# Output products of a hybrid decoder step: from marks along the recurrence to groups of three, ordered both ways by columns

## The chip, the core and the metric

One core of a Trainium2 chip runs one program. The metric is the device time of one execution in microseconds (us). Its engines are named as in the profile: PE (TensorE, with PEld for its weight loads), DVE (VectorE), ACT (ScalarE), POOL (GpSimd) and SP (SyncE, whose queue issues most DMAs here). Each engine takes its instructions in the order in which they stand in the program.

## The reference

One layer of a decoder. The input is normalised and projected, and the columns of the projection go to four groups of heads and a gate. Only the third group (RWKV-7) and the end matter here:

```
def step(S, inp):
    r_t, w_t, k_t, v_t, kk_t, a_t = inp
    sa = jnp.einsum('bhij,bhj->bhi', S, -kk_t)
    S = (S * w_t[:, :, None, :] + sa[..., None] * (kk_t * a_t)[:, :, None, :]
         + v_t[..., None] * k_t[:, :, None, :])
    return S, jnp.einsum('bhij,bhj->bhi', S, r_t)
...
o = jnp.concatenate([oa, ob, oc, od], axis=-1) * jax.nn.silu(gate)
y = x + rms_norm(jnp.einsum('bte,ed->btd', o, w_out), norm_post)
```

The prompt has 2048 tokens; a sample group of 8 sequences of 8 tokens goes through the same weights. The width is 1024, of which the recurrence has 256 (4 heads of 64).

## The kernel before, in words

The first two thirds of the program (input projection, attention, the other head groups) are not touched; the instructions of every engine stand there in the same order before and after. The last part, from about 1250 us of the trace on, is the one that counts: the recurrence and the output projection.

**The recurrence** runs over 16 blocks of 128 tokens, each as two chunks of 64. The generator `rw_prompt` (L1446) gives its steps out one by one. For block i they are: `rw_chain(i)` (L1312), the products that carry the state from chunk to chunk; `rw_tri(i+1)` (L1273), the rest of the triangular inverse of the next block; `rw_norm(i)` (L1397), the group norm of block i, which ends in `out_prep` (L1532), the scaling of token tile i into two f16 halves `o_h`; and `front(i+2)`, which is `rw_prep` (L1105), `rw_mats` (L1182) and `rw_base` (L1252) of the block after the next.

**The round trip to DRAM.** `rw_mats` ends with a small table of diagonal blocks, `r_de` (L1214, DVE). SP writes it to a DRAM tile `zd` (L1217) and reads it back spread over the partitions into `r_zr` (L1221). `rw_base` inverts the 16x16 blocks with it: 15 pairs of small DVE instructions, `r_x16w` (L1262) and `r_x` (L1263), each pair on the result of the one ahead.

**The chain.** For each chunk PE makes `rc` from state `r_Z` and `r_W` (8 products), ACT copies `r_gs`, PE multiplies by `r_TT` (4), ACT scales the result back into `r_Z`, PE multiplies by `r_BK` (4), DVE adds the decayed state (L1372, the new `r_Z`), and PE makes the output with `r_ET` (4), which ACT copies to `r_y`.

**The output** (`out_tile`, L1568) of a tile of 128 tokens is 48 products `acc<-wo,o_h` (L1584) of 512 columns: two halves of 512 output columns, each 8 steps k of three f16 products. ACT scales and squares each half (`o_y`, `o_j`), DVE makes the norm (`o_ss`, `oq`, `o_y`), POOL adds the input (`o_x`, L1599), SP stores.

**What sets the order.** The framework places each engine's instructions by a model of time of its own, which orders whatever the program leaves free. The program adds edges with `issue_after`: the instructions in the block come behind a given one on the same engine. `rw_chain` appends the last product of each of its steps to a list, `spine` (`mark`, L1321), and the three products of a step k of an output tile come behind an entry of that list:

```
ins = spine[(KT * g + k) * len(spine) // (2 * KT)] if spine else None
```

The edge goes one way: nothing holds a product of the recurrence behind an output product. In the loop (L1864) tile i-2 goes out in iteration i, from the second iteration on, after the step of `rw_chain`; one step of the sample's recurrence (`rw_sample`, L1439) follows each of the first five steps of the prompt's. Tiles 14, 16 (the sample's 64 tokens) and 15 are left for the end, in this order.

Of the kernel before, what the change touches and what calls it, by code (L numbers as in the profile page):

```python
# [23 lines left out]
P = 128  # L24
# [12 lines left out]
class Marked:  # L37


    def __init__(self, eng):  # L40
        self.eng, self.done = eng, []

    def matmul(self, *a, **k):
        r = self.eng.matmul(*a, **k)
        self.done.append(r.ins)
        return r

    def transpose(self, *a, **k):
        r = self.eng.transpose(*a, **k)
        self.done.append(r.ins)  # L50
        return r


class Part:


    def __init__(self, ctx, tc, ins, outs):
# [3 lines left out]
        self.PE = Marked(nc.tensor)  # L61
# [1250 lines left out]
    def rw_chain(self, b, S=None):  # L1312
# [8 lines left out]
        mark = lambda ins: smp or self.spine.append(ins.ins)  # L1321
# [13 lines left out]
        for q in range(b.ch):  # L1335
# [3 lines left out]
            for k in range(2):  # L1339
# [7 lines left out]
                mark(ins)  # L1347
# [7 lines left out]
            mark(ins)  # L1355
# [5 lines left out]
            if not smp:  # L1361
# [7 lines left out]
                mark(ins)  # L1369
# [6 lines left out]
            mark(ins)  # L1376
# [69 lines left out]
    def rw_prompt(self, pool):  # L1446

        bs = {}
        self.spine = []
# [118 lines left out]
    def out_tile(self, i, h, sc, pool, psum, spine=()):  # L1568
# [7 lines left out]
        for g in range(2):  # L1576
            sl = slice(512 * g, 512 * g + 512)
            a = psum.tile([P, 512], F32, name="acc", bufs=ACB)
            c = 0
            for k in range(KT):  # L1580
                ins = spine[(KT * g + k) * len(spine) // (2 * KT)] if spine else None
                for e, f in ((0, 0), (0, 1), (1, 0)):
                    with self.tc.issue_after(ins) if ins and e == f else ExitStack():
                        nc.tensor.matmul(a[:n].rearrange("p (c n) -> p c n", c=4), h[:, k, e], self.wo[:, 4 * g:4 * g + 4, k, f, :],  # L1584
                                         start=c == 0, stop=c == 3 * KT - 1)
                    c += 1
            y = pool.tile([P, 512], F32, name="o_y", bufs=OB[3])
# [4 lines left out]
        nc.vector.tensor_tensor(ss[:n, 2:3], ss[:n, 0:1], ss[:n, 1:2], op=ALU.add)  # L1592
        nc.vector.tensor_scalar(ss[:n, 2:3], ss[:n, 2:3], 1.0 / D, 1e-6, op0=ALU.mult, op1=ALU.add)
        self.rsqrt(pool, ss[:n, 3:4], ss[:n, 2:3], n, 1, "oq")
        for g, y in enumerate(ys):
            sl = slice(512 * g, 512 * g + 512)
            nc.vector.scalar_tensor_tensor(y[:n], y[:n], ss[:n, 3:4], self.npo[:n, sl], op0=ALU.mult, op1=ALU.mult)  # L1597
# [173 lines left out]
def program(tc, ins, outs):  # L1771
    with ExitStack() as ctx:
# [68 lines left out]
        with ph2:  # L1841
# [22 lines left out]
            for i in range(RB, 16):  # L1864
                mark = len(p.spine)
                n = min(-((t - 14) // (16 - i)), i - LAG - t)
                for k in range(4):
                    next(seq, 0)
                    if k in SK:
                        next(smp, 0)  # L1870
# [110 lines left out]
```

## Time and profile before

| what | value |
|---|---|
| median of 3 runs | 1844.46 us (1842.14 to 1845.57) |
| the profiled execution, its own time | 1846.33 us |
| span of its trace | 1844.5 us |
| busy over the span | PE 1497.3 us (81%), DVE 1448.1 (79%), ACT 902.1 (49%), POOL 811.6 (44%) |
| granted clock of TensorE, mean | 0.881 of 2.4 GHz |

The shares are means over stages with different limits. What a change in the last stage is worth has to be read from the waits of that stage.

### The profile page before, as it was taken

What the parts mean: (1) busy time and instruction counts of PE and PEld (TensorE: products, weight loads), DVE (VectorE), ACT (ScalarE), POOL (GpSimd) and SP (SyncE); (2) the same over time, 40 slices, a digit from 0 to 9 for tenths busy, and PEclk for the clock granted to TensorE, in tenths of its full rate; (3) what the DMA queues carried; (4) which work ended last, traced back from release to release, by engine and by line L of the source; (5) the groups of instructions that cost most, each with busy time, mean ns of one, the idle gap of its engine ahead of it and who ended that gap; (6) DMA issues with size and microseconds to landing.
All of it is one profiled execution on the core that took longest, in us unless ns stands there. A gap on an engine that the chain in (4) does not pass through costs nothing.

```text
span 1844.5 us, 33323 instructions
## 1 busy us (share of the span) xinstructions
PE 1497.3 (81%) x10956; PEld 844.9 (46%) x10956; DVE 1448.1 (79%) x4619; ACT 902.1 (49%) x2211; POOL 811.6 (44%) x887
## 2 busy tenths in 40 slices
PE   4889888987789788878894899657688887887887
PEld 2445644444344344434442456446455454554443
DVE  7797639988899899889896754376878887888865
ACT  3455746655556566657772222243344454444333
POOL 3441326736668877443344454261324333333312
PEclk9999998999899899989996999875777887887889
DMA  4422144575445655464447877635223233333221
GB/s 147 128 91 93 28 116 117 125 149 117 111 111 139 152 141 146 106 145 115 86 104 199 274 250 238 205 96 163 73 66 100 81 105 93 92 86 102 66 72 58
DMA packets 300898, 225.33 MB, mean 122 GB/s; under 512 B 192531, under 2 KB 248565, under 8 KB 300213
## 3 DMA queue, kind: packets, MB, share of 16 engines
q1 hardware_dynamic: 288388, 184.85, 37.4%
q10 hardware_dynamic: 8496, 24.76, 4.7%
q0 software_dynamic: 3840, 13.61, 2.6%
q8 instruction: 86, 1.41, 0.3%
q14 instruction: 88, 0.71, 0.1%
HBM read 130.04 MB, written 53.24 MB: 99 GB/s over the span
## 4 chain that ended last, share of the span: by engine, by line
DVE 34%; PE 21%; DMA 15%; issue 8%; POOL 4%; ACT 3%; SPq 1%; ACTq 0%; POOLq 0%; DVEq 0%
PE acc L206 7%; DMA r_zr<-zd 5%; DVE a_mx L365 4%; PE acc L1584 4%; DVE a_e L389 4%; DMA a_wt<-a_w 3%; DVE r_x L1263 2%; DVE r_x16w L1262 2%; DVE a_w L395 2%; DMA zd<-r_de 2%; PE ss L511 2%; DVE r_W L1177 1%; PE pf L530 1%; POOL a_e L388 1%; POOL a_w L395 1%
## 5 line engine op out<-in xcount | busy, mean ns | idle before, releaser
L206 PE MATMUL acc<-hT,w 128*128 128x512 f16 (+1 forms) x3120 | 633.6, 353 | 24.7 <-ACT pst L640 4.3
L206 PEld LDWEIGHTS <-w 128*128 128x128 f16 x3120 | 269.7, 101 | 322.3 <-issue 66.8
L368 ACT ACTIVATE a_e<-s,a_mx,sig 128x512 f32<-128x512 f32 (+3 forms) x320 | 226.9, 715 | 122.6 <-DVE a_mx L366 106.4
L1584 PE MATMUL acc<-wo,o_h 128*128 128x512 f16 (+1 forms) x816 | 225.1, 422 | 1.2 <-ACT o_y L1588 0.6
L365 DVE TENSOR_REDUCE a_mx<-s 128x1 f32<-128x512 f32 (+3 forms) x320 | 186.3, 599 | 23.4 <-PE s L361 18.7
L388 POOL TENSOR_SCALAR a_e<-a_e,a_al 128x512 f32<-128x512 f32 (+3 forms) x160 | 114.6, 731 | 148.6 <-DVE a_al L384 119.4
L389 DVE SCALAR_TENSOR_TENSOR a_e<-a_e,a_al 128x512 f32<-128x512 f32 (+3 forms) x160 | 149.3, 948 | 9.2 <-POOL a_e L388 9.0
L361 PE MATMUL s<-kh,qh 128*128 128x512 f16 (+3 forms) x320 | 105.7, 359 | 38.2 <-ACT a_e L368 35.0
L402 PE MATMUL pv<-vtok,a_wt 128*128 128x128 f16 x544 | 70.0, 230 | 64.6 <-DMA a_wt<-a_w 57.9
L392 ACT CAST a_w<-a_e 128x512 f16<-128x512 f32 (+3 forms) x160 | 86.3, 557 | 69.9 <-DVE a_e L389 63.5
L1584 PEld LDWEIGHTS <-o_h 128*128 128x128 f16 (+1 forms) x816 | 76.6, 105 | 95.1 <-issue 26.3
L395 POOL TENSOR_TENSOR a_w<-a_e,a_w 128x512 f16<-128x512 f32 (+3 forms) x80 | 90.0, 1128 | 64.4 <-ACT a_w L392 62.4
L1262 DVE TENSOR_TENSOR r_x16w<-r_zr,r_x 128x60 f32<-128x60 f32 (+18 forms) x255 | 58.8, 231 | 67.0 <-DMA r_zr<-zd 63.8
L1599 POOL TENSOR_TENSOR o_x<-o_y,o_x 128x512 f32<-128x512 f32 (+1 forms) x33 | 48.4, 1487 | 121.4 <-DVE o_y L1597 84.7
L402 PEld LDWEIGHTS <-a_wt 128*128 128x128 f16 x544 | 52.2, 104 | 91.4 <-DMA a_wt<-a_w 76.1
L395 DVE TENSOR_TENSOR a_w<-a_e,a_w 128x512 f16<-128x512 f32 (+2 forms) x80 | 76.9, 964 | 2.7 <-ACT a_w L392 2.7
L170 POOL TENSOR_TENSOR hT<-hf,hT 128x512 f16<-128x512 f32 (+1 forms) x36 | 36.5, 1022 | 88.3 <-ACT hT L168 88.2
L403 PE MATMUL pv<-vtok,a_wt 128*128 128x64 f16 x544 | 66.1, 202 | 0.0
L1263 DVE TENSOR_TENSOR r_x<-r_x,r_x16w 128x60 f32<-128x60 f32 (+18 forms) x255 | 62.4, 245 | 3.4
L368 ACT ACTIVATION_READ_ACCUMULATOR a_e<-s,a_mx,sig 128x1 f32 x320 | 64.0, 200 | 0.0
L366 DVE TENSOR_SCALAR a_mx<-a_mx,sig 128x1 f32<-128x1 f32 x320 | 59.8, 201 | 0.4
L511 PE MATMUL ss<-kv,qbd 128*32 128x256 f32 x256 | 52.5, 415 | 6.7 <-DMA kv<-in_ckv 6.5
(552 smaller groups left out, 3378.0 us busy)
## 6 DMA issues: line engine op xcount, KB each, us to landing
kv<-in_ckv SPq DMA_DIRECT2D x128, 256.0 KB
w<-in_w_in ACTq DMA_DIRECT2D x20, 512.0 KB
pc<-pst SPq DMA_DIRECT2D x40, 256.0 KB
xw<-in_xT SPq DMA_DIRECT2D x16, 512.0 KB
w<-in_w_out ACTq DMA_DIRECT2D x16, 512.0 KB
sg<-pst SPq DMA_DIRECT2D x32, 256.0 KB
r_X<-pc SPq DMA_DIRECT2D x16, 512.0 KB
r_zr<-zd SPq DMA_DIRECT2D x16, 512.0 KB
```

The lines of the kernel that those rows point to most:

```text
L206: self.nc.tensor.matmul(acc[:, :n], w16[:, k, a, :], h[:, k, e, :], start=(c == 0), stop=(c == 3 * KT - 1))
L361: ins = nc.tensor.matmul(s[:, :kn], q[:, c], kh[:, c, k0:k0 + kn], start=True, stop=True)
L365: nc.vector.tensor_reduce(mx[:, p, c:c + 1], s[:, :kn], axis=AX.X, op=ALU.max, negate=True)
L368: nc.scalar.activation(e[:, :kn], s[:, :kn], AF.Exp, scale=sig, bias=mx[:, p, c:c + 1], accum_out=l[:, p, c:c + 1])
L388: nc.gpsimd.tensor_scalar(e1[:, :kn], e1[:, :kn], al[:, p, 1:2], 0.0, op0=ALU.mult, op1=ALU.add)
L389: nc.vector.scalar_tensor_tensor(e0[:, :kn], e0[:, :kn], al[:, p, 0:1], e1[:, :kn], op0=ALU.mult, op1=ALU.add)
L395: eng.tensor_tensor(w[:, kn:], e0[:, :kn], w[:, :kn], op=ALU.subtract)
L402: ins = nc.tensor.matmul(pv[:, :P], wt[:, j], v, start=kt == 0, stop=kt == qb, skip_group_check=True)
L511: ins = nc.tensor.matmul(sp[g:g + 32, 256 * j:min(256 * j + 256, n)], self.qbd[:, m, s].rearrange("p a q -> p (a q)"), rhs, start=True, st ...
L1262: XV.tensor_tensor(w[:, :, :m], zr[:, k, :, k + 1:], x[:, :, k:k + 1].to_broadcast([P, nu, m]), op=ALU.mult)
L1263: XV.tensor_tensor(x[:, :, k + 1:], x[:, :, k + 1:], w[:, :, :m], op=ALU.add)
L1584: nc.tensor.matmul(a[:n].rearrange("p (c n) -> p c n", c=4), h[:, k, e], self.wo[:, 4 * g:4 * g + 4, k, f, :], start=c == 0, stop=c == 3 * ...
```

## The change

- `Marked`, the wrapper of PE that the recurrence's products go through, counts the columns of the products that it issues. With a generator `fill` of output products set by `begin`, it draws one group from it for every `step` columns. A group comes behind the product issued last (`self.PE.last`), and the next product of the recurrence comes behind the group (`gate`). `flush` draws what is left.
- `out_tile` no longer issues anything: it gives two generators, one for each half of the tile, which yield after each group of three products, and a function `rest` with the norm and the store. The two halves have a PSUM buffer each (before: two buffers of one name).
- The loop sends out tile i-1 (before: i-2) in iteration i: the first half between the products of `rw_chain` (a group per 300 columns), the second between those of `rw_tri`, `rw_norm` and `front` (a group per 590 columns; 220 in iteration 14, 30 in iteration 15). Tiles 16 and 15 are left for the end.
- The sample's recurrence is issued whole at the end of iteration 0.

```diff
 class Marked:
+    def begin(self, fill, step):
+        self.fill, self.cols, self.step, self.gate = fill, 0, step, fill and self.last
+
+    def issue(self, op, out, a, k):
+        with self.tc.issue_after(self.gate) if self.gate else ExitStack():
+            r = op(out, *a, **k)
+        self.gate = None
+        self.cols += math.prod(out.shape[1:])
+        self.last = r.ins
+        while self.fill and self.cols >= self.step:
+            self.cols -= self.step
+            self.gate = next(self.fill, None)
+            if self.gate is None:
+                self.fill = None
         return r
...
-    def out_tile(self, i, h, sc, pool, psum, spine=()):
+    def out_tile(self, i, h, sc, pool, psum):
...
-        for g in range(2):
-            sl = slice(512 * g, 512 * g + 512)
-            a = psum.tile([P, 512], F32, name="acc", bufs=ACB)
+        def half(g):
+            a = psum.tile([P, 512], F32, name=f"acc{g}", bufs=1)
             c = 0
             for k in range(KT):
-                ins = spine[(KT * g + k) * len(spine) // (2 * KT)] if spine else None
                 for e, f in ((0, 0), (0, 1), (1, 0)):
-                    with self.tc.issue_after(ins) if ins and e == f else ExitStack():
+                    with self.tc.issue_after(self.PE.last) if e == f else ExitStack():
...
+                if k < KT - 1:
+                    yield ins.ins
...
             for i in range(RB, 16):
-                mark = len(p.spine)
-                n = min(-((t - 14) // (16 - i)), i - LAG - t)
-                for k in range(4):
+                halves = out(i - 1) if i else (None, None, lambda: None)
+                p.PE.begin(halves[0], PACE[0])
+                next(seq, 0)
+                p.PE.flush()
+                p.PE.begin(halves[1], PACE[1 + max(i - 13, 0)])
+                for k in range(3):
+                    if i == 15 and k == 0:
+                        p.out_prep(16)
                     next(seq, 0)
...
+                p.PE.flush()
+                halves[2]()
+                drain(smp)
...
+PACE = (300, 590, 220, 30)
```

The edges move instructions on all engines. Two places on PE and one on DVE follow.

PE, a block in the middle of the prompt before, from the end of the front (`r_prk`, `r_xv`, then `rw`, `hsel` of the block after it) to the transposes of the norm (`r_yc`) and the chain's second step (`r_gs,r_TT`):

```order
L44 MATMUL ra<-r_prk,selh 64x128 x4
L49 MATMUL ra<-ident,r_xv 128x128 x2
L44 MATMUL ra<-r_X,rw_15071 32x128 x4
L44 MATMUL rl<-r_X_17157,r_NA 32x32 x8
L44 MATMUL ra<-r_L,rw_15073 128x128 x2
L44 MATMUL ra<-hsel,r_sq 128x2 x2
L44 MATMUL rl<-r_TT,r_H_17179 32x32 x8
L44 MATMUL ra<-r_L,rw_15073 128x128 x2
L49 MATMUL rl<-ident,r_yc 128x128 x2
L44 MATMUL rc<-r_gs,r_TT 64x64 x4
```

The same products of a middle block in the change, after the last products of `rw_tri`:

```order
L48 MATMUL rl<-r_X_19254,r_NA 32x32 x3
L48 MATMUL rl<-ident,r_yc 128x128 x2
L1594 LDWEIGHTS o_h
L1594 MATMUL acc_19267<-wo,o_h 128x512
...
L48 MATMUL ra<-r_X,rw_15071 32x128 x4
L48 MATMUL rl<-r_TT,r_H_19280 32x32 x8
L1561 MATMUL rl<-o_mx,onec 128x1
L48 MATMUL ra<-r_L,rw_15073 128x128
```

Before, the front's first products (`ra<-r_X,rw`, `r_L`, `hsel`) stand ahead of the norm's transposes `r_yc`; in the change they stand behind them, with a group of three in between, and the tile's `o_mx` stands ahead of `r_L`. This repeats in every block from the second to the fourteenth.

PE, the chain's steps in the change (before, the 4 products of a step stand together, and output products only between steps):

```order
L48 MATMUL rc<-r_gs,r_TT 64x64 x2
L48 MATMUL rc<-r_Z,r_BK 64x64 x3
L1594 LDWEIGHTS o_h
L1594 MATMUL acc_17099<-wo,o_h 128x512
...
L48 MATMUL rc<-r_Z,r_BK 64x64
L48 MATMUL rc<-r_Z,r_W 64x64
L48 MATMUL rc<-r_Z,r_ET 64x64 x3
```

The groups now stand inside the steps: three products before, and one behind, in the step with `r_BK`.

DVE, from `r_de` on, a middle block before:

```order
L1214 TENSOR_REDUCE r_de<-r_dg 128x64
L1409 TENSOR_REDUCE r_nm<-r_y 128x4
L1413 SCALAR_TENSOR_TENSOR r_yc<-r_nm,r_y 128x256
L1243 TENSOR_TENSOR r_sv<-r_xv,ra 128x256
L1592 TENSOR_TENSOR o_ss<-o_ss 128x1
L1593 TENSOR_SCALAR o_ss<-o_ss 128x1
L1294 TENSOR_TENSOR r_TT<-r_XY,rl 128x256
L99 TENSOR_SCALAR o_ss<-o_ss 128x1
L1420 TENSOR_REDUCE r_nss<-r_nsq 128x4
L1281 STREAM_TRANSPOSE r_X_18809<-r_TT 128x256
L100 TENSOR_SCALAR o_ss<-o_ss 128x1
L1421 TENSOR_SCALAR r_nss<-r_nss 128x4
```

And a middle block in the change:

```order
L1231 TENSOR_REDUCE r_de<-r_dg 128x64
L1260 TENSOR_TENSOR r_sv<-r_xv,ra 128x256
L1607 TENSOR_TENSOR o_ss<-o_ss 128x1
L1279 TENSOR_TENSOR r_x16w<-r_zr,r_x_19926 128x60
L1608 TENSOR_SCALAR o_ss<-o_ss 128x1
L1280 TENSOR_TENSOR r_x_19926<-r_x_19926,r_x16w 128x4x15
L116 TENSOR_SCALAR o_ss<-o_ss 128x1
L1279 TENSOR_TENSOR r_x16w<-r_zr,r_x_19926 128x4x14
```

Before, the norm of one block, the end of `rw_tri` and the norm of an output tile stand between `r_de` and the first instruction that reads `r_zr`, which is the 29th behind `r_de` in the block shown. In the change it is the third, in this block and in nearly all others.

## Rows read from the trace of the kernel before

**Rows 1.** The page's chain that ended last, whole span: shares by engine.
```profile
DVE 34%; PE 21%; DMA 15%; issue 8%; POOL 4%; ACT 3%; SPq 1%; ACTq 0%; POOLq 0%; DVEq 0%
```
**Rows 2.** Busy time by stage (us, with instructions), then granted clock, DMA share, GB/s.
```profile
core 0: us, PE busy (x) PEld busy (x) DVE busy (x) ACT busy (x) POOL busy (x), PEclk, DMA share, GB/s
1258.00:1311.00 53.00, 36.56 (x374) 30.22 (x375) 41.25 (x169) 17.12 (x53) 12.12 (x21) 0.53 0.52 156
1311.00:1753.00 442.00, 364.55 (x3210) 214.45 (x3211) 366.42 (x1431) 186.05 (x522) 154.67 (x217) 0.81 0.31 87
1753.00:1799.00 46.00, 38.97 (x355) 19.70 (x354) 28.10 (x128) 18.91 (x53) 8.83 (x11) 0.89 0.23 73
1799.00:1844.50 45.50, 33.01 (x151) 14.95 (x150) 25.60 (x98) 15.63 (x36) 10.41 (x7) 0.92 0.17 58
```
**Rows 3.** Waits of DVE from 1311 to 1753 us: us, times, longest.
```profile
DVE r_x16w L1262 <- DMA r_zr<-zd: 53.4, 13, 6.6
DVE o_o L1526 <- DMA o_o<-od: 2.3, 3, 1.0
```
**Rows 4.** SP's queue, timeline: start, us, the writes of r_de (five of 17).
```profile
1249.47 0.33 SPq L1217 DMA_DIRECT2D zd<-r_de  x1
1276.84 0.33 SPq L1217 DMA_DIRECT2D zd<-r_de  x1
1310.77 0.34 SPq L1217 DMA_DIRECT2D zd<-r_de  x1
1344.23 0.33 SPq L1217 DMA_DIRECT2D zd<-r_de  x1
1752.61 0.33 SPq L1217 DMA_DIRECT2D zd<-r_de  x1
```
**Rows 5.** The chain that ended last, one round trip: start, us, what.
```profile
1514.36 0.58 DVE r_de L1214
1514.96 2.22 DMA zd<-r_de
1517.25 6.73 DMA r_zr<-zd
1524.00 0.22 DVE r_x16w L1262
```
**Rows 6.** DVE, timeline: instructions that waited, with idle time and its releaser.
```profile
1271.67 0.45 DVE L1281 STREAM_TRANSPOSE r_XY<-r_XY 128x256 f32<-128x256 f32 x1 [0.79 <-POOL r_XY L1270]
1285.29 0.42 DVE L1420 TENSOR_REDUCE r_nss<-r_nsq 128x4 f32<-128x256 f32 x1 [0.48 <-ACT r_nsq L1419]
1787.96 0.63 DVE L1423 TENSOR_TENSOR r_yc<-r_yc,r_nrs 128x256 f32<-128x256 f32 x1
1791.60 0.43 DVE L1431 TENSOR_TENSOR r_yo<-r_yo,r_sv 128x256 f32<-128x256 f32 x1 [2.68 <-ACT r_yo L1429]
1813.60 0.16 DVE L1548 TENSOR_TENSOR o_mx<-o_mx 128x1 f32<-128x1 f32 x1 [0.64 <-ACT o_j L1547]
```
**Rows 7.** PE, timeline: products that DVE waits for, and two groups of three.
```profile
1790.28 0.44 PE L49 MATMUL rl<-ident,r_yc 128*128 128x128 f32 x2
1517.80 0.61 PE L44 MATMUL ra<-hsel,r_sq 128*128 128x2 f32 x4
1536.63 1.71 PE L44 MATMUL ra<-r_W,r_F 64*128 64x128 f32 x16
1535.88 0.82 PE L1584 MATMUL acc<-wo,o_h 128*128 128x512 f16 x3
1521.91 1.46 PE L1584 MATMUL acc<-wo,o_h 128*128 128x512 f16 x3
```
**Rows 8.** ACT, groups from 1300 us on: busy us, mean ns of one, idle before.
```profile
L1561 ACT ACTIVATE o_h<-o_o,o_sc 128x1024 f16<-128x1024 f32 (+1 forms) x17 | 19.1, 1123 | 36.1 <-DVE o_sc L1559 33.4 <-DVE r_Dp L1132 2.7
L1148 ACT ACTIVATE r_sq<-r_X,vec 128x128 f32<-128x128 f32 x24 | 8.3, 398 | 1.2 <-PE ra L44 1.2
L1529 ACT ACTIVATE o_j<-o_o 128x768 bf16<-128x768 f32 (+1 forms) x16 | 13.1, 820 | 0.3
L1206 ACT COPY r_NA<-ra 64x256 f32<-64x256 f32 x28 | 10.2, 364 | 10.7 <-PE ra L44 10.4
```
**Rows 9.** The page's DMA issues: KB each.
```profile
r_zr<-zd SPq DMA_DIRECT2D x16, 512.0 KB
```
**Rows 10.** PE, timeline: the last products, tiles 16 and 15.
```profile
1822.73 10.09 PE L1584 MATMUL acc<-wo,o_h 128*128 128x512 f16 x46 [0.29 <-ACT o_y L1588]
```

More of the change, by code (lines that the diff above doesn't have):

```diff
@@ L37, with __init__, matmul, transpose @@
 class Marked:
[L40 to L45, printed above, removed]
-        return r
[L48 to L51, printed above, removed]
+    def __init__(self, eng, tc):
+        self.eng, self.tc, self.fill, self.cols, self.step, self.last, self.gate = eng, tc, None, 0, 1, None, None
+    def begin(self, fill, step):
[11 more added lines that the diff above has]
+                self.fill = None
+        return r
+    def matmul(self, out, *a, **k):
+        return self.issue(self.eng.matmul, out, a, k)
+    def transpose(self, out, *a, **k):
+        return self.issue(self.eng.transpose, out, a, k)
+    def flush(self):
+        for _ in self.fill or ():
+            pass
+        self.fill = self.gate = None
 class Part:
@@ L1591, in out_tile, with rest @@
             ys.append(y)
[L1592 to L1597, printed above, removed]
-            eng = nc.vector if i == 15 and g else nc.gpsimd
-            eng.tensor_tensor(x[:n, sl], y[:n], x[:n, sl], op=ALU.add)
-        nc.sync.dma_start(self.o["y"][t0:t0 + n], x[:n])
+            yield ins.ins
+        def rest():
+            nc.vector.tensor_tensor(ss[:n, 2:3], ss[:n, 0:1], ss[:n, 1:2], op=ALU.add)
+            nc.vector.tensor_scalar(ss[:n, 2:3], ss[:n, 2:3], 1.0 / D, 1e-6, op0=ALU.mult, op1=ALU.add)
+            self.rsqrt(pool, ss[:n, 3:4], ss[:n, 2:3], n, 1, "oq")
+            for g, y in enumerate(ys):
+                sl = slice(512 * g, 512 * g + 512)
+                nc.vector.scalar_tensor_tensor(y[:n], y[:n], ss[:n, 3:4], self.npo[:n, sl], op0=ALU.mult, op1=ALU.mult)
+                eng = nc.vector if i == 15 and g else nc.gpsimd
+                eng.tensor_tensor(x[:n, sl], y[:n], x[:n, sl], op=ALU.add)
+            nc.sync.dma_start(self.o["y"][t0:t0 + n], x[:n])
+        return half(0), half(1), rest
     def rwkv_sample_consts(self, pool):
@@ L1854, in program, with out @@
             smp = p.rw_sample(rw, sm)
[L1856 removed]
+            def out(t):
                 if t not in p.prep:
                     p.out_prep(t)
[L1859 to L1863 removed]
+                return p.out_tile(t, *p.prep.pop(t), p.opool, ops)
             for i in range(RB, 16):
[L1865 to L1883 removed]
+                halves = out(i - 1) if i else (None, None, lambda: None)
[6 more added lines that the diff above has]
+                        p.out_prep(16)
+                    next(seq, 0)
+                p.PE.flush()
+                halves[2]()
+                drain(smp)
+            for t in (16, 15):
+                halves = out(t)
+                drain(halves[0])
+                drain(halves[1])
+                halves[2]()
 LEAD = 1500
@@ L1921 @@
 SSB = 3
-LAG = 1
 ES = 999
```

34 lines of the change are left out of this document (3 added, 31 removed).

## The prediction

> **What bounds the kernel now.** I read the page's chain of waits first, since it says which engine ended the program [rows 1]: DVE has the largest share, 34%, then PE 21% and DMA 15%. It covers the whole span, so the next view is the busy time by stage [rows 2]. From 1311 to 1753 us, 13 of the 16 blocks, PE works 364.55 and DVE 366.42 of 442 us: neither is full, and PE works at a granted clock of 0.81. What fills the rest on DVE is in the view of its waits for that stretch [rows 3]: 53.4 us, 13 times, always the first instruction that reads `r_zr`, for the DMA that brings it. SP's timeline gives the pace: the write of `r_de` to `zd` comes at 1344.23 for block 3 and at 1752.61 for block 15 [rows 4], 12 intervals in 408.4 us, 34.03 us each. Per block DVE works 366.42/13 = 28.2 us and waits 53.4/13 = 4.1 us for `r_zr`; 1.7 us are small waits. So the stage goes by the order of DVE's instructions: it is busy or waits for the round trip.
>
> The chain that ended last shows one round trip [rows 5]: `r_de` is done at 1514.94, the write lands 2.2 us later, the read takes 6.73, and the first `r_x16w` runs at 1524.00. That is 9.06 us, of which DVE waits 4.1 on average, since it makes the norm, the end of `rw_tri` and the output's norm in the other 5. These are the 28 rows that stand between `r_de` and `r_x16w` in the order before.
>
> **The change part by part.**
>
> *The round trip's cover.* The change removes and adds no arithmetic: DVE keeps its 28.2 us per block. But two-way edges put PE into the program's order. The front's first product `ra<-r_X,rw` now stands behind the norm's transposes `r_yc`, so DVE has to make `r_yc` of block i before anything of the front of i+2. The norm can then no longer stand behind that front's `r_de`. In the new order `r_de` is followed by `r_sv` and one `o_ss`, and then by `r_x16w`, which needs the transfer issued just before. Instructions of these sizes took 0.43 and 0.16 us [rows 6], so 9.06 - 0.6 = 8.5 us per block lie open. I take 8.5; PE's and ACT's work under it does not help, since the decayed state `r_Z` stands behind this wait on DVE too, and with it the rest of the chain and its groups. The transfer itself could change with what shares the queues: it is 512 KB [rows 9], and no other size of it is in the trace, so I leave it.
>
> On the size of the wait a rule can be set against rows 5. The Trainium skill ("DMA: Bandwidth & Descriptors", "Anatomy of one DMA — SWDGE (gpsimd) path") fits a transfer, on the path of POOL's software queue, by about 2.0 us and its bytes at 436 GB/s; as an estimate this gives some 2.1 us for `zd`, 3.2 us for `r_zr`, 5.3 us in all instead of 9.06, and a forecast about 45 us lower. The trace has the very transfer and disagrees for the read (6.73 us), and the sum goes by the trace.
>
> *What the norm and the front now wait for.* Before, DVE had an instruction of another step for nearly every gap. Now the steps of DVE stand one behind the other, base (i+2), norm (i), `out_prep`, front (i+3), and each answer of PE, ACT or POOL is waited for. Per block, by the nearest rows:
> - `r_XY` for POOL: 0.79 us [rows 6], on a block that had little else to do.
> - `r_nss` for ACT: 0.48 us was the wait there [rows 6]. ACT's queue now has `o_j` (0.82 us) [rows 8] of the same tile ahead of `r_nsq`; between 0.5 and 1.6, I take 1.0.
> - `r_yc` to `r_yo`: the transposes and ACT's copy left DVE idle for 2.68 us in the last block, where nothing else was to do [rows 6]; from the transposes' start at 1790.28 [rows 7] to `r_yo` at 1791.60 it is 1.3. I take 1.3, as some of the output's norm stands in between.
> - `o_mx` for `o_j`: 0.64 us [rows 6].
> - `o_sc` to `r_ss`: `o_h` (1.12 us) now stands ahead of two `r_sq` (0.40 each) on ACT [rows 8], and PE's `hsel` follows (0.61 us) [rows 7]: 2.5 us.
> - The products `ra<-r_W,r_F` (1.71 us) with a group of three ahead (0.82 us, 1.46 in the slow case) [rows 7] and ACT's copy (0.36 us) [rows 8]: 2.9 us.
> - `r_TT`, `oq` and `r_Dp`, for which no row shows a wait of this kind: nothing at best, the 0.5 us of `r_nss` each as the nearest; 1.5 us.
>
> The sum is 8.5 + 0.8 + 1.0 + 1.3 + 0.6 + 2.5 + 2.9 + 1.5 = 19.1 us, and with DVE's 28.2 the interval is 47.3 us. With only the first lower bounds (8.5, 0.8, 0.5, 0, 0.6, 1.1 for `o_h` alone, 1.7, 0) it is 41.4.
>
> *PE's clock.* PE's 364.55/13 = 28.0 us per block would fill 59% of 47 us, and 82% before. In the stretch where the trace has PE at 69%, 1258 to 1311 us, the granted clock was 0.53, half speed for most of it [rows 2]. I expect part of the stage at half speed. The parts that DVE waits for and that are PE's (some 5.5 us of the 19.1) grow by up to 0.81/0.53, which is 2.9 us; I take **50 us** per block. Half speed throughout, with groups of 1.46 us and more in front of each awaited product, bounds it at 56.
>
> *Twelve blocks*: 12 x (50 - 34.03) = **+192 us**.
>
> *The first blocks and the sample.* From the write of block 1 (1249.47) to that of block 3 (1344.23) [rows 4] it was 94.8 us, with the sample's `zd` in between. Less two intervals of 34.03 the sample cost 26.7. Before it was woven into five steps of the prompt's; now it is issued whole behind iteration 0, with its own round trip. I put it at the same 26.7, and at up to 9 more if its round trip lies open. The first of the two blocks has no output tile: 45 us, the other 50. Together 122: **+27 us**.
>
> *The tail.* From the write of block 15 to the end it was 91.9 us. Tile 14 no longer goes out last: 46 products took 10.09 us [rows 10], 0.22 each, so 48 are 10.5 us. They now stand inside the last chain, whose products wait behind them; there PE has 45.5 - 33.0 = 12.5 idle us at most [rows 2]. The gain is between 0 and 10.5; I take **-5 us**.
>
> *Queues.* Nothing is added to SP's or POOL's. On SP the store of a tile, which waits for POOL's `o_x`, stands behind the transfers `r_zr` and `r_xv` of the front, so it doesn't hold them. PSUM gives each half one buffer: a half's first group waits for ACT's reads of the half one tile ago, a whole interval earlier. Both cost nothing while a block takes more than PE's 28 us.
>
> **The sum.** 192 + 27 - 5 = 214 us on the profiled execution's 1846.33 us: 2060. The median shown is 1.9 us below that execution, so I forecast **2058 us**.
>
> **Rivals.**
>
> *Only the transfer shows.* If the waits on ACT and PE stay short, an interval is 28.2 + 8.5 + 1.7 = 38.4 us: 12 x 4.4 = 53 us, some 9 for the first two blocks, nothing for the tail, so 1907. For it: POOL and ACT have much room. Against it: DVE's next instruction now mostly stands on the answer of the one ahead.
>
> *It ends faster.* The groups inside the steps are there to fill PE's short gaps. If they set the pace, the awaited products find PE warm, the clock goes from 0.81 to near 1, and DVE's 28.2 us plus 0.8 for small waits is the interval: 13 x (34.0 - 29.0) = 65 us less, and with -10 at the tail 1770 us. It decides from the point where at least 9 us of DVE's work stand between `r_de` and `r_x16w`; the new order shows 0.6, and 5 didn't suffice before. The Trainium skill speaks for this side ("TensorE: Matmul & The Clock Gate", "HAM oscillation — how this bites in real kernels"): a loop that leaves PE idle for a wait in each round starts each round cold. By that rule the wait of 8.5 us would as well cool PE anew in every block, the opposite, and the 0.53 of rows 2 leans that way.
>
> *No change.* The engines' work is the same, and if the open waits only take the place of DVE's old ones, 4.1 + 1.7 us, the time stays at 1844. It needs gaps that the rows of the order contradict.
>
> *Half speed throughout.* An interval of 56 gives 12 x 22 = 264 us and 35 at the beginning: about 2140.
>
> **How the numbers follow.** Serial steps at 42 to 54 us have 0.80, half speed throughout 0.06, only the transfer 0.06, no change 0.03, faster 0.05. The lower end of the range is the lower bound of the interval: 12 x (42 - 34.03) = 96, +15 and -7 for the ends, 1950. The upper is the half speed case with a little more, 2150. The likeliest case lies inside, with part of the fourth; what is out is the transfer alone, no change and faster. About 0.2% is what a measurement of this kernel can tell from no change: faster 0.05, within 0.03, slower 0.92.
>
> **What would show it.** Right: the writes of `r_de` stand 45 to 54 us apart; DVE waits for `r_zr` 13 times or more, some 8 us each, 110 us in the stage where it was 53; `r_ss`, `r_yo` and `o_mx` appear among DVE's waits, for PE and ACT; DVE's own busy time per block stays near 28 us; PE's granted clock in the stage falls below 0.81. Wrong: intervals below 40 us with `r_zr` as DVE's only large wait (the transfer alone); a PE over 90% busy at a clock near 1 (the faster case); a wait of PE for the PSUM halves, or of the front for a store on SP, which I put at nothing; a first part much over 122 us, if the sample's round trip isn't covered by anything.

## The result and the profile after

The changed kernel takes **2233.78 us** (median of 4 runs, 2229.41 to 2234.28), the kernel before 1845.01: a ratio of 1.2097 with a 95% interval from 1.2064 to 1.213. The direction was right. The size was not: 2058 us was forecast, and the time lies above the range's upper end of 2150. The profiled execution took 2229.41 us with a span of 2227.6.

The page's chain of the changed kernel, shares by engine, where DVE led in [rows 1]:

```profile
PE 35%; DVE 24%; DMA 11%; issue 8%; ACT 6%; POOL 5%; SPq 1%; ACTq 0%; DVEq 0%; POOLq 0%
```

PE has changed places with DVE. The changed kernel's SP timeline shows where the time lies:

```profile
1246.16 0.34 SPq L1234 DMA_DIRECT2D zd<-r_de  x1
1382.66 0.34 SPq L1234 DMA_DIRECT2D zd<-r_de  x1
2109.59 0.33 SPq L1234 DMA_DIRECT2D zd<-r_de  x1
```

These are the writes of blocks 1, 3 and 15, to be read against [rows 4]. From block 1 to 3 it is 136.5 us (before 94.8), from block 3 to 15 726.9 us or 12 intervals of 60.58 (before 34.03), and to the end of the span 118.1 (before 91.9). The three add 41.7 + 318.5 + 26.1 = 386.3 us; the first write came 3.3 us earlier, which makes up the 383.1 us between the two profiled executions.

Busy time by stage, columns as in [rows 2], the same three stretches:

```profile
1246.16:1382.66 136.50, 86.20 (x678) 55.60 (x677) 77.84 (x300) 35.23 (x105) 23.63 (x41) 0.61 0.30 89
1382.66:2109.59 726.93, 502.92 (x3056) 260.46 (x3053) 386.87 (x1355) 178.01 (x503) 147.43 (x204) 0.63 0.18 51
2109.59:2227.65 118.06, 79.75 (x432) 36.12 (x430) 44.26 (x181) 27.96 (x71) 16.39 (x16) 0.72 0.11 37
```

Per interval DVE is busy 386.87/12 = 32.2 us and PE 41.9, at a granted clock of 0.63. DVE's waits from 1382.66 to 2109.59 us (us, times, longest) answer to [rows 3]:

```profile
DVE r_W L1224 <- ACT r_NA L1223: 61.9, 24, 3.8
DVE r_x16w L1279 <- DMA r_zr<-zd: 52.2, 12, 5.5
DVE r_Z L1385 <- PE rc L48: 40.9, 12, 4.2
DVE r_yo L1443 <- ACT r_yo L1441: 28.0, 12, 3.8
DVE o_ss L1607 <- ACT o_j L1602: 21.9, 12, 1.8
DVE r_sv L1260 <- PE ra L48: 21.9, 12, 2.3
DVE r_ss L1169 <- PE ra L48: 20.3, 12, 2.7
DVE r_XY L1298 <- POOL r_XY L1287: 15.4, 11, 1.5
DVE r_nss L1432 <- ACT r_nsq L1431: 14.8, 12, 1.3
DVE r_nm L1421 <- ACT r_y L1393: 7.9, 10, 1.3
```

Where one wait for a transfer was nearly all, the view now has fourteen kinds, of which these are the nine largest and `r_nm`; each comes once or twice in nearly every block. One round trip in DVE's timeline of the changed kernel (start, us, idle before and its releaser):

```profile
1739.56 0.58 DVE L1231 TENSOR_REDUCE r_de<-r_dg 128x64 f32<-128x256 f32 x1
1742.24 0.42 DVE L1260 TENSOR_TENSOR r_sv<-r_xv,ra 128x256 f32<-128x256 f32 x1 [2.09 <-PE ra L48]
1744.48 0.16 DVE L1607 TENSOR_TENSOR o_ss<-o_ss 128x1 f32<-128x1 f32 x1 [1.83 <-ACT o_j L1602]
1749.03 0.22 DVE L1279 TENSOR_TENSOR r_x16w<-r_zr,r_x 128x60 f32<-128x60 f32 x1 [4.38 <-DMA r_zr<-zd]
...
1751.69 0.60 DVE L1385 TENSOR_TENSOR r_Z<-rc,r_sd 64x128 f32<-64x128 f32 x2
```

The trip takes 8.9 us, of which DVE idles 2.09 + 1.83 + 4.38 = 8.3. The first chunk's `r_Z` stands behind it on DVE. PE's timeline of the same block shows the groups and the waits:

```profile
1744.92 0.82 PE L1594 MATMUL acc<-wo,o_h 128*128 128x512 f16 x3
1752.02 0.48 PE L48 MATMUL rc<-r_Z,r_W 128*64 128x64 f32 x2 [3.91 <-DVE r_Z L1385]
1753.05 1.46 PE L1594 MATMUL acc<-wo,o_h 128*128 128x512 f16 x3
1773.31 1.46 PE L1594 MATMUL acc<-wo,o_h 128*128 128x512 f16 x3
1788.65 1.12 PE L133 MATMUL ra<-ident,r_rs 128*64 128x128 f32 x8 [6.57 <-DVE r_rs L128]
1793.39 1.46 PE L1594 MATMUL acc<-wo,o_h 128*128 128x512 f16 x3
```

Ahead of the wait of 3.91 us a group takes 0.82 us, behind it 1.46. And the chain of this stretch (1740 to 1802 us) has output products as its largest part, 23.6% of 62 us, that is 14.6 us. The first line below is its shares by line, the others are four of its pieces in a row:

```profile
by line: PE acc L1594 23.6%; DMA r_zr<-zd 11.9%; PE rc L48 8.8%; PE ra L48 8.7%; PE rl L48 5.5%; DMA zd<-r_de 4.7%; DVE r_W L1194 4.2%; issue 4.1%; DVE r_de L1231 1.9%; PE ra L133 1.8%; ACT o_h L1572 1.7%; DVE r_x16w L1279 1.6%; ACT o_j L15
...
1773.38 1.39 PE acc L1594 x3
1774.77 0.97 PE rl L48 x8
1775.74 1.28 PE acc L1594 x3
1777.02 1.00 PE ra L48 x8
```

From 1772.86 to 1780.62 us the chain stays on PE, which works off its order; what ACT waits for at the end of it is `ra<-r_L,rw`. Such groups stand ahead of that, so they are on the path.

### The profile page after: what moved, and what is told of

Its sections match the earlier page's. It is cut to its first block, busy times and chain, and to the rows that moved or that the text cites. A ratio compares the mean times of both kernels' runs of the same rounds, so it can differ in the third digit from the quotient of the medians.

```text
span 2227.6 us, 33356 instructions
## 1 busy us (share of the span) xinstructions
PE 1691.7 (76%) x10956; PEld 914.0 (41%) x10956; DVE 1488.9 (67%) x4619; ACT 900.5 (40%) x2211; POOL 810.0 (36%) x887
## 3 DMA queue, kind: packets, MB, share of 16 engines
q1 hardware_dynamic: 288388, 184.85, 31.1%
## 4 chain that ended last, share of the span: by engine, by line
PE 35%; DVE 24%; DMA 11%; issue 8%; ACT 6%; POOL 5%; SPq 1%; ACTq 0%; DVEq 0%; POOLq 0%
PE acc L1594 11%; PE acc L223 6%; DMA r_zr<-zd 5%; PE rc L48 4%; PE ra L48 4%; DVE a_mx L382 3%; DVE a_e L406 3%; DMA a_wt<-a_w 3%; PE rl L48 2%; DVE r_W L1194 2%; PE ss L528 1%; DVE a_w L412 1%; PE pf L547 1%; POOL a_e L405 1%; DMA zd<-r_de 1%
## 5 line engine op out<-in xcount | busy, mean ns | idle before, releaser
L1594 PE MATMUL acc<-wo,o_h 128*128 128x512 f16 (+1 forms) x816 | 315.4, 519 | 4.9 <-ACT o_h L1572 3.7
L405 POOL TENSOR_SCALAR a_e<-a_e,a_al 128x512 f32<-128x512 f32 (+3 forms) x160 | 114.7, 732 | 147.8 <-DVE a_al L401 118.1
L1378 POOL TENSOR_TENSOR r_sd<-r_Z,r_Dp 64x128 f32<-64x128 f32 x64 | 26.5, 414 | 306.2 <-DVE r_Z L1385 303.0
L1279 DVE TENSOR_TENSOR r_x16w<-r_zr,r_x 128x60 f32<-128x60 f32 (+14 forms) x255 | 64.2, 252 | 82.1 <-DMA r_zr<-zd 77.7
L412 POOL TENSOR_TENSOR a_w<-a_e,a_w 128x512 f16<-128x512 f32 (+3 forms) x80 | 89.8, 1125 | 63.2 <-ACT a_w L409 61.2
L1180 POOL TENSOR_SCALAR r_kf<-r_tha,rwv 128x128 f32<-128x128 f32 (+1 forms) x34 | 18.2, 535 | 224.1 <-ACT r_tha L1155 224.1
L48 PE MATMUL ra<-r_W,r_F 64*128 64x128 f32 x256 | 56.0, 449 | 39.3 <-DVE r_F L1197 38.6
L133 PE MATMUL ra<-ident,r_rs 128*64 128x128 f32 (+1 forms) x136 | 18.2, 415 | 88.3 <-DVE r_rs L128 86.2
L48 PE MATMUL rc<-r_Z,r_W 128*64 128x64 f32 x512 | 44.4, 278 | 52.4 <-DVE r_Z L1385 52.4
L1223 ACT COPY r_NA<-ra 64x256 f32<-64x256 f32 x32 | 11.7, 366 | 171.3 <-PE ra L48 171.1
```

What stands on the lines that cost most here:

```text
L48: r = op(out, *a, **k)
L405: nc.gpsimd.tensor_scalar(e1[:, :kn], e1[:, :kn], al[:, p, 1:2], 0.0, op0=ALU.mult, op1=ALU.add)
L412: eng.tensor_tensor(w[:, kn:], e0[:, :kn], w[:, :kn], op=ALU.subtract)
L1279: XV.tensor_tensor(w[:, :, :m], zr[:, k, :, k + 1:], x[:, :, k:k + 1].to_broadcast([P, nu, m]), op=ALU.mult)
L1594: ins = nc.tensor.matmul(a[:n].rearrange("p (c n) -> p c n", c=4), h[:, k, e], self.wo[:, 4 * g:4 * g + 4, k, f, :], start=c == 0, stop=c ...
```

## The experiments

Three causes were to be told apart: ORDER (two-way edges force PE's order, so DVE's steps stand one behind the other), PATH (groups stand ahead of awaited products) and CLOCK (half speed as a cause of its own). Below, "interval" is the mean of the twelve between the writes of blocks 3 and 15; the lines are the view of busy time by stage for these twelve, with the columns of [rows 2]. A time without a ratio is that of one execution; thirteen executions of the kernel before lay between 1839.38 and 1854.05 us, so a difference of some 10 us in a total tells nothing. The intervals of the change and of two runs below that leave its middle blocks as they are lie between 60.6 and 61.2 us.

**No back edges.**

```diff
-        with self.tc.issue_after(self.gate) if self.gate else ExitStack():
-            r = op(out, *a, **k)
+        r = op(out, *a, **k)
```

> The change with its back edges taken out: an output group still comes behind the recurrence's last product, but no product of the recurrence has to wait for a group. Three theories stand. ORDER: the back edges force PE into the program's order, DVE's steps stand one behind the other, and each answer of another engine is waited for. PATH: the groups themselves stand ahead of products that DVE and ACT wait for (in the changed kernel's chain 'PE acc' is 23.6% of a 62 us interval, 14.6 us). CLOCK: PE idles more, falls to half speed and every product of the chain takes twice as long. In this kernel 1 to 21 rows of DVE stand between r_de and r_x16w (before 18 to 31, change 3), so ORDER expects an interval between two writes of r_de of 38 to 44 us and 1900 to 2000 us in all. PATH expects 34 to 37 us and at most 1890, since no group is held in front of anything. CLOCK expects a granted clock over 0.75 in the stage with either.

1919.51 us, 1.0388 times the kernel before (1.0307 to 1.0469), interval 39.25. The back edges are over 300 of the 389 us. It is not yet the kernel before; that DVE has less work standing behind `r_de` here (1 to 21 rows, before 18 to 31) may be why. ORDER's interval holds, PATH's 34 to 37 does not.

**Back edges in the chain alone.**

```diff
-        with self.tc.issue_after(self.gate) if self.gate else ExitStack():
+        with self.tc.issue_after(self.gate) if self.gate and self.both else ExitStack():
...
+                p.PE.both = True
                 p.PE.begin(halves[0], PACE[0])
...
+                p.PE.both = False
                 p.PE.begin(halves[1], PACE[1 + max(i - 13, 0)])
```

> Back edges for the first half of a tile alone (the groups inside the chain's steps), none for the half that goes between the inverse, the norm and the front. DVE then mixes the norm of a block with the front of another again (their Newton steps alternate in its order), but only 4 rows stand between r_de and r_x16w. ORDER: DVE's busy time per block falls from 32.2 back to about 28.5, the waits r_ss, r_yo, r_nss and o_mx go, r_zr stays open with some 7 us: interval 42 to 46 us instead of 60.6, about 2020 us. PATH: the eight groups of the chain stay on the path, half of the 14.6 us goes: 52 to 55 us, about 2140. CLOCK: the granted clock stays near 0.63.

2055.72 us, interval 48.1, DVE busy 28.7 us per block:

```profile
1352.74:1930.05 577.31, 430.78 (x3052) 231.57 (x3050) 344.22 (x1354) 183.15 (x503) 142.26 (x205) 0.70 0.23 64
```

Between the two expectations. DVE's busy time fell back as ORDER said, and the waits that it named all but went (`r_ss` 1.3 us in all twelve intervals, `r_nss` 0.3, `o_mx` 0.4, `r_yo` none in the view). But the interval fell by 12.5 us, not by 15 to 19, and DVE now waits 3.9 us per block for the chain's products before the front's `r_W`. Both halves of the change cost.

**One product in three.**

```diff
-                for e, f in ((0, 0), (0, 1), (1, 0)):
+                for e, f in ((0, 0),):
...
```

> The changed kernel with one product in each group in place of three (the first f16 product of a step k; the two that carry the low parts are left out, so the output is coarser). All edges and the order of the recurrence stay. ORDER: the groups are not what is waited for, interval 57 to 60 us, about 2190 us. PATH: two thirds of the 14.6 us per block go, some 10 us: interval 50 to 51 us, and about 2090 us. CLOCK: PE has less to do, granted clock no higher than 0.63, which eats part of what PATH gives back.

2105.47 us, interval 52.8, above PATH's range and below ORDER's. PE's clock was 0.53, lower still. Two thirds of the products were worth 7.8 us per block, of PATH's 10; by a straight line no products at all would leave 48.9.

**Strict order alone, in the kernel before.**

```diff
-        r = self.eng.matmul(*a, **k)
+        with self.tc.issue_after(self.done[-1]) if self.strict else ExitStack():
+            r = self.eng.matmul(*a, **k)
...
```

> The kernel before with one thing added: in the last part each product of the recurrence (the sample's too) comes behind the product of the recurrence issued before it. Output tiles go out as before (tile i-2, marks that go one way), so no group is held in front of a product by an edge. DVE's order then has r_x16w as the second row behind r_de, as in the change. ORDER: most of the loss shows here, interval 54 to 60 us, 2100 to 2200 us. PATH: only the open round trip and small waits, interval 40 to 46 us, 1930 to 2000 us. CLOCK: 0.63 to 0.70 in the stage with ORDER.

2124.83 us, interval 53.5, just under ORDER's range, early part 135.2, tail 96.4. No edge holds a group ahead of anything, and yet 19.5 us per block are lost. The twelve intervals, and DVE's largest wait in them:

```profile
1384.13:2026.67 642.54, 392.29 (x3050) 237.40 (x3048) 379.14 (x1355) 182.39 (x502) 156.84 (x204) 0.68 0.20 57
DVE r_x16w L1264 <- DMA r_zr<-zd: 100.0, 12, 9.0
```

That is 8.3 us per block, 4.2 more than before. DVE's busy time is 31.6 us, and all its waits in the view add up to 20.1. ORDER is shown as a cause by itself.

**The sample woven in as before.**

```diff
                 next(seq, 0)
+                next(smp, 0)
...
                     next(seq, 0)
+                    next(smp, 0)
...
-                drain(smp)
```

> The changed kernel with the sample's recurrence woven in as before: one of its steps behind each of the first five steps of the prompt's, in place of all of them at the end of iteration 0. Measured is the time from the write of r_de of block 1 to that of block 3: 94.8 us before, 136.5 in the change, 135.2 in the kernel before with strict order (whose sample is woven). SAMPLE (issuing it whole costs the 42 us): 95 to 110 us, total about 2200. ORDER (the strict order costs it, wherever the sample stands): 128 to 140 us, total 2220 to 2240.

2218.03 us; from block 1 to 3 it is 119.3 us, between the two expectations. Issuing the sample whole costs 17 of the 42 us there; the rest stays with order and groups.

**Tile 14 at the end.**

```diff
-                halves = out(i - 1) if i else (None, None, lambda: None)
+                halves = out(i - 1) if 0 < i < 15 else (None, None, lambda: None)
...
-            for t in (16, 15):
+            for t in (14, 16, 15):
```

> The changed kernel, but tile 14 goes out at the end, ahead of tiles 16 and 15, in place of between the products of the last block's steps. Measured is the time from the write of r_de of block 15 to the end: 91.9 us before, 118.1 in the change, 96.4 with strict order and no back edges. PATH (the 48 products stand ahead of awaited ones at half speed, some 20 us, and cost 10.5 us at the end): 104 to 110 us, total about 2220. If the tail's loss came from the order of the other engines: 115 to 120 us, or more by the 10.5 us.

2221.80 us; the tail is 99.4 us in place of 118.1. Taking the 48 products out of the last block's steps gained 18.7 us net, more than PATH said.

**Groups in PE's waits, order free between.** `put(n)` draws n groups at once and sets the gate.

```diff
+        PE.put(8)
         pbc = bank()
...
+        PE.put(3)
         for h, r in HALF:
             o = HALF[1 - h][1]
...
+                PE.put(5 if q == 0 else 0)
                 for h, r in HALF:
                     dst = b.Z[r, 1, 0, h] if q == 0
...
```

> Groups put where PE of the changed kernel waited longest, with back edges there alone: five groups behind the products with r_BK of a block's first chunk (PE waited 3.9 us there for r_Z), eight ahead of those with r_rs (6.6 us), three ahead of those of r_W and r_F (2.5 us); the r_rs products now go through the wrapper too. Between these points the recurrence's order is free; 7 to 25 rows of DVE stand between r_de and r_x16w. ORDER and PATH together: the order is nearly that of before, the groups lie in waits: interval 34 to 38 us, total 1840 to 1900. If a few large gates alone already fix PE's order so far that DVE waits: 42 to 48 us, 1960 to 2030.

1912.49 us, interval 38.2: just outside the first expectation. Fewer gates in better places cost 4 us per block against the kernel before, of which sending out tile i-1 takes 3 by itself (below).

**The same with strict order.**

```diff
-        with self.tc.issue_after(self.gate) if self.gate else ExitStack():
+        ins = self.gate or self.strict and self.last
+        with self.tc.issue_after(ins) if ins else ExitStack():
...
```

> As the run with groups in PE's long waits, but each product of the recurrence comes behind the one issued before it, so that PE's order is the program's, as in the change; 13 rows of DVE (small ones) stand between r_de and r_x16w. Only the place of the groups differs from the change (60.6 us per interval). PATH: the groups go off the path, interval 48 to 52 us, total 2060 to 2110. ORDER alone: 57 to 60 us, 2190 and more. CLOCK: with the groups in PE's longest gaps its granted clock rises over 0.70; if the clock were a cause of its own, the interval would fall below the 48.9 us to which the changed kernel and the one with a third of the products point for no groups at all.

2042.19 us, interval **46.3**, granted clock 0.71:

```profile
1394.38:1949.67 555.29, 389.17 (x3052) 231.21 (x3050) 372.80 (x1356) 184.50 (x502) 155.76 (x204) 0.71 0.23 66
```

With all products and a strict order, the other place of the groups is worth 60.6 - 46.3 = 14.3 us per block. But it is not the groups alone: DVE's order, which the edges leave to the framework, moved with them. In eleven of the twelve blocks the first chunk's `r_Z` (both halves or one), which stands behind the round trip in the change, now stands ahead of the wait for it, with more of the output's norm:

```profile
1676.33 0.59 DVE L1400 TENSOR_TENSOR r_Z<-rc,r_sd 64x128 f32<-64x128 f32 x2 [0.43 <-PE rc L52]
1681.40 0.22 DVE L1293 TENSOR_TENSOR r_x16w<-r_zr,r_x 128x60 f32<-128x60 f32 x1 [4.49 <-DMA r_zr<-zd]
```

DVE's waits under the trip (`r_zr` 47.3, `r_sv` 0.8 in twelve intervals) are 4.0 us per block in place of 8.0, and PE's chain runs on beside it. So some 4 of the 14.3 us are the trip. The interval even lies below the 48.9; the trip, and the clock (0.71 in place of 0.53 to 0.63), may have a part in that.

**Added products at the wait for `r_rs`.**

```diff
+            PE.gate = PE.gate or PE.last
...
         V.tensor_scalar(ss[:n], pss[:n, :4], 1e-24, None, op0=ALU.max)
+        if getattr(self, "warm", False) and not smp:
+            for k in range(16):
+                with self.tc.issue_after(self.PE.last):
+                    nc.tensor.matmul(pss[:, P:].rearrange("p (c n) -> p c n", c=3),
...
```

> The changed kernel with 16 products more per block (384 columns, into unused columns of a bank of PSUM, read by nobody) at the place where PE waits longest, 6.6 us, for r_rs; at half speed they take about 5.8 us, so they fit in the wait. The two last products with rw now come ahead of those with hsel, so that nothing awaited stands behind the added ones. In the changed kernel the twelve intervals go with the granted clock: 55.8 us at 0.77, 57.3 at 0.71, 60.4 to 61.5 at 0.61 to 0.64, 62.5 at 0.58. CLOCK (half speed is a cause of its own): the granted clock rises to 0.75 or more and the interval falls to 53 to 57 us although PE has more to do. If the clock only goes along with what else makes an interval long: 60 to 62 us, or more by what the added products overrun.

2232.32 us, interval 60.9, clock 0.69: no gain. The clock stayed under the 0.75 that CLOCK asked for, so this run does not decide. PE still idled 4.3 us for `r_Z`, and the chain behind it ran at half speed.

**Added products in the chain.**

```diff
+                if getattr(self, "warm", False) and q == 0 and b.blk > 1:
+                    for k in range(32):
+                        with self.tc.issue_after(PE.gate or PE.last):
+                            PE.gate = nc.tensor.matmul(self.spare,
...
```

> The changed kernel with 32 products more per block (256 columns, into unused columns of PSUM, read by nobody), behind the products with r_BK of a block's first chunk, where PE waited 3.9 us for r_Z and after which its products took twice as long (a group of three 1.46 us in place of 0.82). At full speed the added ones take about 3.5 us, so they fit in the wait. In the run with added products at the wait for r_rs PE still stood idle for 4.30 us at this place, and the groups behind it took 1.46. CLOCK: the groups behind this place take 0.82 us again, granted clock 0.72 or more, interval 53 to 57 us. If the clock only goes along: groups at 1.46, or at 0.82 with an interval of 60 to 62 us.

2217.61 us, interval 60.1. PE's timeline of this kernel, behind the added products:

```profile
1758.52 0.82 PE L1601 MATMUL acc<-wo,o_h 128*128 128x512 f16 x3
1766.84 0.48 PE L48 MATMUL rc<-r_Z,r_ET 64*64 64x64 f32 x4 [3.15 <-DVE r_Z L1392]
1767.25 1.46 PE L1601 MATMUL acc<-wo,o_h 128*128 128x512 f16 x3
```

The second chunk's products up to `r_BK` took 7.0 us in place of 11.6. But DVE's second `r_Z` now stands behind all 30 instructions of its base, so PE idled 3.15 us for it, and the next groups took 1.46 us again. DVE's waits over the twelve intervals show where the gain went:

```profile
DVE r_nm L1428 <- ACT r_y L1400: 32.9, 12, 2.9
DVE r_Z L1392 <- PE rc L48: 7.6, 3, 4.4
```

The wait for `r_Z` fell from 40.9 to 7.6 us, and that for the chain's output, `r_y`, rose from 7.9 to 32.9. The wait moved more than it went.

**Added products at all long waits.**

```diff
+                    for k in range(32 - 8 * q):
...
+            for k in range(16):
+                with self.tc.issue_after(PE.gate or PE.last):
+                    PE.gate = nc.tensor.matmul(pbc[:, 2:4],
...
```

> The changed kernel with added products (read by nobody) at all of PE's long waits of a block: 32 and 24 of 256 columns behind the products with r_BK of the first and the second chunk (waits for r_Z), 16 of 384 ahead of those with r_rs, 16 of 256 ahead of those of r_W and r_F. The run with added products at the first place alone had its chain at full speed (groups of three 0.82 us) and gained nothing: DVE's 30 instructions of the base ran beside the chain and ended later, PE then waited 3.15 us for the next r_Z, and the inverse, the norm and the front behind it were at half speed again. Here these too should be at full speed: granted clock 0.85 or more. CLOCK: in the changed kernel's twelve intervals the time goes from 62.5 us at 0.58 to 55.8 at 0.77, so 52 to 56 us here, about 2130. If the clock only goes along with something else: 59 to 61 us.

2197.15 us, interval 58.0, clock 0.84. Two of the twelve intervals:

```profile
1616.16:1677.54 61.38, 49.03 (x343) 28.05 (x342) 31.96 (x113) 15.03 (x42) 13.01 (x17) 0.78 0.18 53
1852.02:1906.24 54.22, 43.12 (x343) 25.55 (x342) 32.29 (x113) 14.80 (x42) 13.06 (x17) 0.91 0.20 59
```

The gain of 2.5 us is smaller than CLOCK's, but the added products cost something too: those ahead of `r_W,r_F` took 3.31 us at half speed in a wait of 2.5. In the best of these blocks, at 0.91, it is still 54.2 us, far above the 46.3; and the worst takes 61.4 us at 0.78, where one of the change took 55.8 at 0.77, so the granted clock alone does not set the length. The clock is a part at most, some 2.5 us by the mean and some 6 by the best block; how much exactly stays open.

**The read split, in the change.** One transfer of 128 KB, then one of 384 KB, in two tiles.

```diff
-        b.zr = til("zr", [P, 16, 4, 16])[:, :, :nu]
+        b.zr = [til("zr", [P, 4, 4, 16])[:, :, :nu], til("zs", [P, 12, 4, 16])[:, :, :nu]]
+        for k, m, zr, q in ((0, 4, b.zr[0], nc.sync), (4, 12, b.zr[1], nc.sync)):
+            z0 = zd[k, 0, 0:1]
...
```

> The changed kernel with the round trip's read in two transfers (a quarter, then the rest), as in the split kernel before, which gained 2.4 us per interval. The open round trip (r_zr, with r_sv and o_ss under it) is some 8 us of the changed kernel's 60.6: if it lies on the path by its whole length, as I forecast, the interval falls by 2.5 to 4 us, to 56.5 to 58 us. If other waits take its place (for o_j and the products behind it): 59.5 to 61 us.

2187.23 us, interval 57.2, which is 3.4 us less: the open round trip lies on the path, as the prediction had it.

**Tile i-1 alone, in the kernel before.**

```diff
-LAG = 1
+LAG = 0
```

> One part of the change alone, in the kernel before: tile i-1 goes out in iteration i in place of i-2; marks as before, one way, sample woven. ORDER and PATH: no recurrence product is held, interval 33 to 36 us, and the tail loses tile 14 (up to 10.5 us of its 91.9): 1830 to 1860 us. If putting out the newer tile alone makes the framework's order worse (15 rows between r_de and r_x16w in place of 29 in some blocks): 36 to 39 us, 1870 to 1900.

1875.97 us, 1.0161 times (1.011 to 1.0212). The tail gains 5 us (87.0), the intervals lose more (37.2). This part of the change costs by itself.

**The read split, in the kernel before.** The edit is that of the split above.

> The kernel before, with the round trip's read in two transfers on the same queue: the first four rows of every block of 16 (128 KB) and then the other twelve (384 KB), in two tiles, so that the first r_x16w waits for a quarter of the data. ORDER (the open round trip is what bounds the kernel before, 4.1 us per block): if the first piece lands in 3 to 4 us in place of 6.7, the wait falls by 2 to 4 us a block, interval 30.5 to 32.5 us, total 1790 to 1825. If a transfer costs most of its 6.7 us whatever its size, or the second piece is waited for in place of the first: 1840 to 1860.

**1807.34 us, 0.9797 times the kernel before (0.9758 to 0.9837)**, faster than both kernels. Interval 31.6; DVE's waits over the twelve:

```profile
DVE r_x16w L1263 <- DMA r_zr<-zd: 10.1, 8, 2.8
DVE r_x16w L1263 <- DMA r_zs<-zd: 2.7, 2, 1.5
```

12.8 us are left of the 49.2 that the kernel before waits for `r_zr` in its twelve intervals.

**Both together.**

> The split read together with tile i-1 going out in iteration i, both in the kernel before. If both parts gain and do not touch each other: the sum of the two gains. If the order of DVE (9 and 20 rows between r_de and r_x16w in turn) keeps less cover than the split kernel's own 17 to 30: 1840 to 1900.

1847.20 us, ratio 1.0012 (0.9989 to 1.0035). This is the second expectation. Tile i-1 alone lost 29 us and the split alone gained 40; their sum would be a gain of 11, and both together changed nothing that can be measured. The interval is 35.3 us, some 2 below tile i-1 alone.

## Why the prediction was wrong, and where it was right

**Right in the main: what bounds it.** DVE's steps stand one behind the other, the round trip lies open, and the norm and the front wait for ACT, PE and POOL; but the chain now runs over PE for 35%, where the forecast had DVE's order alone. The 8.5 us for the trip are 8.0 measured (`r_zr` 4.35, `r_sv` 1.83, `o_ss` 1.83, all inside it), not as one wait of 8, but shared by three. The split read shows that it is on the path. `o_mx` (0.6), `r_XY` (0.8, measured 1.3), `r_nss` (1.0, measured 1.2) and `r_ss` (2.5, measured 1.7) were sized about right. The new PSUM buffers cost nothing, as put down: PE's groups show no wait in the twelve intervals.

**Strict order: the waits about right, the total by luck.** With the groups in PE's waits the serial order takes 46.3 us per block, near the forecast 47.3. That agreement is luck: the trip lies open for 4.0 us there and not for 8.5, and DVE is busy for 31.1 us and not for 28.2. The kernel before with strict order has DVE's order of the forecast, with the trip open for 8.6 us (`r_zr` 8.3, `r_sv` 0.2). Its waits in the view, 20.1 us, are near the 19.1 of the sum as a total, though not one by one (`r_Z` 2.6 against none, `r_ss` 0.9 against 2.5). But it takes 53.5 us: DVE's busy time is 31.6 us, and some 1.8 us of small gaps come on top. The order costs 12.2 us of the 26.5 by the first run and 19.5 by the second.

**Wrong: the price of the groups.** The sum let one group of 0.82 us stand in front of one awaited product, and added 2.9 us for the clock: 3.7 us per block. Measured is 7.1 against strict order in the kernel before (60.6 against 53.5), 11.7 by the straight line of one product in three, and 14.3 against the groups in PE's waits (60.6 against 46.3), of which some 4 are the trip; on the chain of one block they are 14.6. No run separates order and groups more sharply, since each run places the groups, and with them DVE's order, in its own way. In the trace it shows as waits that the sum had no term for, or too small a one: `r_Z` for the chain's products 40.9/12 = 3.4 us against none, `r_W` for `r_NA` 5.2 against 2.9, `r_yo` 2.3 against 1.3. In all DVE idles 28.3 us per block, where the sum with its clock term had 22.0; with the busy time below this is the miss per block. The order of PE printed ahead of the prediction had groups inside every step; each of them should have been put into the sum at its place.

**Wrong: DVE's work stays at 28.2 us.** It is 32.2, and 31 to 32 in every kernel with strict order, but 28.7 with back edges in the chain alone. The instructions are the same. Added up one by one, DVE's rows of the twelve intervals come to 34.0 us per block before and 35.2 in the change; 5.8 us of that overlap before, and 2.9 in the change. DVE's timelines show the overlap: first three of the kernel before, where two chains alternate, then three of the changed kernel, where one stands alone.

```profile
1524.14 0.15 DVE L109 TENSOR_TENSOR kq<-r_rs 128x4 f32<-128x4 f32 x1
1524.26 0.22 DVE L1263 TENSOR_TENSOR r_x<-r_x,r_x16w 128x60 f32<-128x60 f32 x1
1524.40 0.15 DVE L110 SCALAR_TENSOR_TENSOR kq<-kq,r_ss 128x4 f32<-128x4 f32 x1
```

```profile
1772.88 0.16 DVE L126 TENSOR_TENSOR nq<-r_nrs 128x4 f32<-128x4 f32 x1
1773.08 0.16 DVE L127 SCALAR_TENSOR_TENSOR nq<-nq,r_nss 128x4 f32<-128x4 f32 x1
1773.27 0.16 DVE L128 SCALAR_TENSOR_TENSOR r_nrs<-nq,r_nrs 128x4 f32<-128x4 f32 x1
```

Alternating, one starts every 0.13 us, ahead of the end of the one before; where each needs the one ahead, every 0.20. That the need for the result is what ends the overlap is not shown; no run tested it by itself.

**Wrong: the ends.** The first blocks took 136.5 us, not 122: the sample, issued whole, costs 17, where at most 9 were put down for its round trip. The tail took 118.1, not 87: the output products were set down as a gain of 5 us there, and they stand in front of the last block's awaited products; moving tile 14 away gives 18.7 back.

The miss adds up for the profiled execution: 12 x (60.6 - 50) = 127, 14.5 in the first blocks, 31 in the tail, less 3.3 us before them, is 169 of 2229 - 2060. The rivals fell: nothing came of the warm PE (clock 0.63), and the transfer was not the only new wait. Half speed throughout was the nearest, but with an interval bounded at 56 it lacked the same terms. The Trainium skill's rule on a loop that goes cold in each round ("TensorE: Matmul & The Clock Gate", "HAM oscillation — how this bites in real kernels") agrees with the trace: groups of 0.82 us ahead of the wait of 3.91 us, 1.46 behind it.

## What to carry to other kernels

An edge that holds an engine's next product behind filler puts that filler on the path wherever the product is awaited; count every group at its place in the order, at the slower clock that the trace shows behind long waits. Filler belongs where the engine already waits for long, and an order that a two-way edge fixes on one engine takes the choice from the others as well. After moving filler, read the other engines' orders again: here DVE's `r_Z` changed sides of the transfer's wait. Before rearranging work to cover a transfer, see whether its first reader needs all of it: here the split read was the only edit that beat the kernel before.

## What was not expected of the hardware

A quarter of the read (128 KB) takes much less than the whole: two pieces of the split kernel's chain, 384 KB behind the write of one block and 128 KB behind that of another, beside 6.73 us for 512 KB in [rows 5] (five pieces of 128 KB in that chain took 2.65 to 3.17 us):

```profile
1361.38 5.36 DMA r_zs<-zd
...
1679.82 2.65 DMA r_zr<-zd
```

And a stretch of PE at full speed need not shorten the block: in the run with added products in the chain, the groups behind them took 0.82 us in place of 1.46 and the interval moved from 60.6 to 60.1 us only. DVE's 30 small instructions beside them set when the next `r_Z` came, and PE waited for it and was slow again behind it.
